# Copying the blocks of u inside DRAM into load order, ahead of the pass that uses them

## The chip, the cores and the metric

The kernel runs on one core of one Trainium2 chip. The metric is the device time of one launch in microseconds (us). The engines are named as in the profile: PE multiplies matrices (PEld is its weight load), DVE and ACT are the vector and scalar engines, POOL works on SBUF and issues the indirect transfers, and SP issues all other DMA transfers. The transfers of SP and of POOL run on the same 16 DMA engines.

## What is computed

One decoder layer on 512 tokens of width 2048, in float32: an input projection, a short convolution and a differential attention side by side, an output projection, and then a product-key expert layer. This last part takes most of the time. Every token chooses 16 of 16,384 experts for each of 8 heads, and every expert is one row of `expert_u` and one row of `expert_v`:

```python
def apply(args):
    xb, ib, gb = args
    u = jnp.take(expert_u, ib, axis=0)
    a = jnp.einsum('thkd,td->thk', u, xb)
    w = (jax.nn.gelu(a.astype(jnp.float32), approximate=False) * gb).astype(xb.dtype)
    vv = jnp.take(expert_v, ib, axis=0)
    return jnp.einsum('thk,thkd->td', w, vv)
```

Both tables are 128 MB (16,384 rows of 8 KB).

## The kernel before

**Stages.** In order of time: the modulation vectors and the q and k columns of the input projection; the v columns (`for g in range(2)`, with `turn`); the convolution columns and the attention heads (`conv`, `head`); the output projection, which also prepares the first 12 blocks of u (`u_ahead`); the projection of the queries onto the key halves (the loop over `w_peer_q`, line 701, below called the key projection), with the top-16 selection on DVE; four blocks of the dense pass between the last selections (`u_block(0)` to `u_block(3)`); the spreading of the gates into `g_dram` (lines 899 to 918, with eight more u blocks); and the dense pass.

**The dense pass.** 352 of the 512 tokens are served densely: all 128 blocks of 128 experts are multiplied with all of these tokens. The other 160 tokens are served by gathers: POOL fetches the chosen rows of `expert_u` and `expert_v` by indirect DMA (line 844, 512 KB each, four buffers `gt`), and DVE multiplies and adds them (lines 853 and 869). Both run beside each other; the gathers are paced by the matmuls.

A block e of the dense pass needs u transposed, so that the width lies on the partitions. `u_load` brings the block to SBUF in 8 transfers of 128 KB each, into a tile `ur` in which partition group s (32 partitions) holds columns s*512 to s*512+511 of the rows, four rows to a partition (line 511):

```python
for b in (0, 2):
    for s in range(4):
        nc.sync.dma_start(t[s * 32:(s + 1) * 32, b:b + 2],
                          expert_u[e * P + b * 32:e * P + b * 32 + 64, s * 512:(s + 1) * 512]
                          .rearrange("(b r) d -> r b d", r=32))
```

DVE then transposes 32x32 squares (line 780, `utf`), ACT and DVE split the result into a high and a low part (lines 88 and 89, `ut`), PE runs 48 matmuls of 352 columns (line 792), and 48 more at line 945, where v (`vr`, one transfer of 512 KB for two blocks and a quarter of the width) is split in the same way (`vs`) and multiplied by the weights `W`. There are two tiles `ur`, so one block is loaded while the one before it is transposed.

The first 12 blocks are different: `u_ahead` transposes them during the output projection and stores them in the DRAM tile `u_dram`, from where one transfer of 1 MB brings each to SBUF (line 773).

**What sets the order.** The framework places the instructions of each engine in an order that it works out itself from the dependencies, with a few orders added by hand. SP issues its transfers strictly in this order: one that has to wait for a buffer holds up all behind it. In addition each transfer from SP takes one of eight completion semaphores in turn and waits, where need be, until the transfer before it on the same semaphore has landed, so at most eight are under way.

**Weights in the earlier stages.** `weights` loads a 512 KB tile `wraw` (four buffers), ACT takes the high part (line 88) and POOL the low part (line 89) into `wsp`, and PE uses it. A free `wraw` buffer thus comes from POOL, and SP waits for it.

Of the kernel before, what the change touches and what calls it, by code (L numbers as in the profile page):

```python
# [78 lines left out]
def hymba_peer(tc, x, c, positions, w_ada, b_ada, norm1_g, w_in, conv_w, q_norm_g, k_norm_g,  # L79
# [18 lines left out]
    with ExitStack() as ctx:  # L98
# [1 line left out]
        y_dram = tc.dram_tile([KC, P, T], F32, name="y_dram")  # L100
        x1_dram = tc.dram_tile([KC, P, T], F32, name="x1_dram")
        g_dram = tc.dram_tile([TD // GB, NK, NK, GB], F32, name="g_dram")
        u_dram = tc.dram_tile([NPRE, P, D], F32, name="u_dram")
        h_dram = tc.dram_tile([TG - P, D], F32, name="h_dram")
        a_dram = tc.dram_tile([P, D], F32, name="a_dram")

# [106 lines left out]
        def ada_later(n):  # L213
            for _ in range(n):
                if later:
                    sec, k0 = later.pop(0)
                    ada(sec, k0, 4)
                    if sec == 4:
                        gain_col(1, 4, k0, 4)


        def weights(w, r0, nk, c0, n, behind=None):
# [164 lines left out]
        for g in range(2):  # L387
            banks = [pm() for _ in range(NT)]
            for kq in range(8):
                qkv_mm(banks, 4 + g, kq * 2, (0, KC - 1))  # L390
            for i in range(NT):
                nc.scalar.activation(vv[:, i, g * 512:(g + 1) * 512], banks[i], AF.Copy)
            turn(2 * g)
            turn(2 * g + 1)
            ada_later(ADA_N.pop(0))
# [51 lines left out]
        def conv(cp):  # L447
            got = []
            for g in (1, 2, 0):
                banks = [pm() for _ in range(2)]  # L450
                for kq in range(4):
                    ws = weights(w_in, kq * 512, 4, g * CONV + cp * 256, 256)
                    for k in range(4):
                        kk = kq * 4 + k
                        for n2 in range(2):
                            for n, (a, b) in enumerate(PASSES):
                                nc.tensor.matmul(banks[n2], ws[:, a, k, n2 * P:(n2 + 1) * P], hT[kk][:, b],  # L457
                                                 start=(kk == 0 and n == 0), stop=(kk == KC - 1 and n == 2))
                for n2 in range(2):
                    if g == 1:  # L460
                        cc = at.tile([P, T], F32, name="cc")
                        nc.scalar.activation(cc, banks[n2], AF.Copy)
                        got.append(cc)
                        continue
                    chn = cp * 2 + n2
                    if g == 2:
                        z = at.tile([P, T + 2], F32, name="cz", bufs=1)
                        nc.vector.memset(z[:, 0:2], 0.0)
                        nc.vector.tensor_tensor(out=z[:, 2:], in0=banks[n2], in1=got[n2], op=OP.mult)
                        y = got[n2]  # L470
                        nc.vector.tensor_scalar(y, z[:, 0:T], ccol[:, 16 + chn:17 + chn], None, op0=OP.mult)
                        for j in (1, 2):
                            wc = ccol[:, 16 + j * 8 + chn:17 + j * 8 + chn]
                            nc.vector.scalar_tensor_tensor(y, z[:, j:T + j], wc, y, op0=OP.mult, op1=OP.add)
                    else:
                        y = got[n2]
                        nc.vector.tensor_tensor(out=y, in0=banks[n2], in1=y, op=OP.mult)
                        nc.sync.dma_start(y_dram[chn], y)
# [210 lines left out]
        for g in range(4):  # L689
            banks = [pm() for _ in range(4)]  # L690
            for kq in range(8):
# [2 lines left out]
                    dense_tokens((g * 8 + kq) * 2 + n, weights.hi)  # L694
                if kq % 2:
                    gathered_tokens((g * 8 + kq) // 2, weights.hi)
                for k in range(2):
                    kk = kq * 2 + k
                    for j in range(4):
                        for n, (a, b) in enumerate(PASSES):  # L700
                            nc.tensor.matmul(banks[j], ws[:, a, k, j * P:(j + 1) * P], h2T[kk][:, b],  # L701
                                             start=(kk == 0 and n == 0), stop=(kk == KC - 1 and n == 2))
# [63 lines left out]
        def u_turn(n):  # L766
# [2 lines left out]
                return  # L769
            if q == 0:  # L770
                UR[0] = up.tile([P, 4, 512], F32, name="ur", bufs=UR_BUFS)
                if e < NPRE:
                    nc.sync.dma_start(UR[0].rearrange("p b d -> p (b d)"), u_dram[e])
                else:
                    u_load(UR[0], e)
            if e < NPRE:
                t = UR[0][:, 2 * q:2 * q + 2].rearrange("p a (c b r) -> p (a c) b r", c=4, b=4)
            else:
# [5 lines left out]
        def u_block(e, behind=None):  # L784
# [15 lines left out]
            if e % 2 == 0:  # L800
# [6 lines left out]
                else:  # L807
                    GE[e // 2] = up.tile([P, 2, TD], F32, name="ge", bufs=GE_BUFS)
            nc.scalar.activation(GE[e // 2][:, e % 2], pa[:, :TD], AF.Gelu)

        held = [scores(qs, i, psV.tile([P, T], F32, name="pv"), gp.tile([P, D // 2], F32, name="gt", bufs=GBUF)[:, 0:T])
                for i in range(NT)]
# [14 lines left out]
            split(W[e // 2], ge)  # L827

        for i in range(NT):
            u_block(i)  # L830
            select(i, 3, held[i])
            finish_select(i)
        tk_ctx.close()
# [63 lines left out]
        with tc.tile_pool(name="gs", bufs=2, side="right") as gs:  # L897
# [3 lines left out]
            for b in range(nb_):  # L901
                gt_ = gs.tile([P, NK, GB], F32, name="gtile")
                for t4 in range(0, GB, 4):
# [12 lines left out]
                        gm = nc.tensor.matmul(pg[:, j], oh[:, 1, j], og[:, j], start=True, stop=True)  # L916
                    nc.scalar.activation(gt_[:, :, t4:t4 + 4], pg.rearrange("p t n -> p n t"), AF.Copy)
                nc.sync.dma_start(g_dram[b], gt_)
                if b >= nb_ - (RUN - NT):
                    u_block(RUN - nb_ + b, behind=gm if b == nb_ - 1 else None)  # L920

# [133 lines left out]
```

## Time and profile before

| | us |
|---|---|
| median of 3 runs (range) | 3523.54 (3519.87 to 3523.54) |
| the profiled execution | 3524.61 |
| span of its instructions | 3522.6 |
| q and k projection, up to | 283 |
| v columns | 283 to 389 |
| convolution and heads | 389 to 772 |
| output projection | 772 to 974 |
| key projection | 974 to 1190 |
| u blocks 0 to 3, last selections | 1190 to 1284 |
| spreading of the gates, u blocks 4 to 11 | 1284 to 1432 |
| dense pass | 1432 to about 3390 |
| end | to 3522 |

How to read it: 2.0 us of the profiled execution lie outside the span. Busy time is time in which an engine executed something; the DMA share is the mean busy share of the 16 DMA engines, and can exceed 1 a little when packets of two queues overlap on an engine. The stage borders come from the first and last matmul of each line.

### The profile page before, as it was taken

What the parts mean: (1) busy time and instruction counts of PE and PEld (TensorE: products, weight loads), DVE (VectorE), ACT (ScalarE), POOL (GpSimd) and SP (SyncE); (2) the same over time, 40 slices, a digit from 0 to 9 for tenths busy, and PEclk for the clock granted to TensorE, in tenths of its full rate; (3) what the DMA queues carried; (4) which work ended last, traced back from release to release, by engine and by line L of the source; (5) the groups of instructions that cost most, each with busy time, mean ns of one, the idle gap of its engine ahead of it and who ended that gap; (6) DMA issues with size and microseconds to landing.
All of it is one profiled execution on the core that took longest, in us unless ns stands there. A gap on an engine that the chain in (4) does not pass through costs nothing.

```text
span 3522.6 us, 49092 instructions
## 1 busy us (share of the span) xinstructions
PE 3223.4 (92%) x18006; PEld 2970.3 (84%) x18006; DVE 2847.1 (81%) x4261; ACT 1220.5 (35%) x1828; POOL 1417.5 (40%) x985
## 2 busy tenths in 40 slices
PE   5888999999998797999999999999999999999985
PEld 4766777677787686899998999889999999999975
DVE  6789766653269999789898888888999898988885
ACT  5232334343264357423232232223233232332221
POOL 2447332254447420134443444333434444444441
PEclk9999999999999899999999999999999999999987
DMA  8864755559722135899999999999999999999984
GB/s 288 286 229 143 254 190 178 183 177 290 252 88 68 61 122 202 264 298 323 305 315 295 310 310 299 300 287 300 306 314 313 298 307 306 326 310 319 299 302 163
DMA packets 425712, 896.34 MB, mean 254 GB/s; under 512 B 40402, under 2 KB 119167, under 8 KB 420735
## 3 DMA queue, kind: packets, MB, share of 16 engines
q1 hardware_dynamic: 333310, 557.62, 52.3%
q0 software_dynamic: 92160, 335.59, 29.3%
q8 instruction: 141, 2.31, 0.3%
q14 instruction: 101, 0.82, 0.1%
HBM read 843.47 MB, written 49.55 MB: 254 GB/s over the span
## 4 chain that ended last, share of the span: by engine, by line
DMA 42%; DVE 28%; PE 15%; issue 9%; POOL 3%; SPq 2%; ACT 1%; DVEq 0%; POOLq 0%; ACTq 0%
DMA ur<-in_expert_u_dram 14%; DMA vr<-in_expert_v_dram 9%; DMA gt<-in_expert_u_dram,idxu 6%; PE pm L457 4%; DMA ada_w<-in_w_ada_dram 4%; DMA gt<-in_expert_v_dram,idxu 4%; DVE gacc L869 3%; DVE utf L780 3%; DVE vs L89 2%; DVE gt L907 2%; DVE gt L853 2%; DVE ut L89 2%; DVE ada_acc L196 2%; PE pm L547 2%; DVE run L196 2%
## 5 line engine op out<-in xcount | busy, mean ns | idle before, releaser
L792 PE MATMUL pa<-hd,ut 128*128 128x352 f32 x6144 | 1077.3, 328 | 63.9 <-DVE ut L89 41.0
L945 PE MATMUL pv<-W,vs 128*128 128x352 f32 x6144 | 1071.4, 328 | 50.6 <-DVE vs L89 27.0
L792 PEld LDWEIGHTS pa<-hd,ut 128*128 128x128 f32 x6144 | 1015.2, 191 | 75.8 <-DVE ut L89 48.4
L945 PEld LDWEIGHTS pv<-W,vs 128*128 128x128 f32 x6144 | 1014.5, 191 | 61.2 <-DVE vs L89 32.7
L89 POOL TENSOR_TENSOR wsp<-wraw,wsp 128x1024 fp32r<-128x1024 f32 x160 | 391.5, 2449 | 562.1 <-ACT wsp L88 530.3
L844 POOL DMA_INDIRECT gt<-in_expert_u_dram,idxu x256 | 343.9, 1344 | 626.4 <-DVE gt L853 309.8
L88 ACT ACTIVATE vs<-vr 128x1024 fp32r<-128x1024 f32 x256 | 271.3, 1060 | 819.2 <-DMA vr<-in_expert_v_dram 365.8
L844 POOL DMA_INDIRECT gt<-in_expert_v_dram,idxu x256 | 340.0, 1328 | 477.9 <-DVE gacc L869 341.5
L853 DVE SCALAR_TENSOR_TENSOR gt<-gt,h2n 128x1024 f32<-128x1024 f32 x320 | 386.2, 1215 | 104.9 <-DMA gt<-in_expert_u_dram,idxu 84.8
L869 DVE SCALAR_TENSOR_TENSOR gacc<-gt,ga_a,gacc 128x1024 f32<-128x1024 f32 x316 | 400.4, 1275 | 73.9 <-DMA gt<-in_expert_v_dram,idxu 48.5
L89 DVE TENSOR_TENSOR vs<-vr,vs 128x1024 fp32r<-128x1024 f32 x256 | 309.8, 1210 | 46.9 <-ACT vs L88 46.7
L88 ACT ACTIVATE ut<-utf 128x1024 fp32r<-128x1024 f32 x232 | 244.0, 1056 | 282.3 <-DVE utf L780 169.6
L780 DVE STREAM_TRANSPOSE utf<-ur 128x1024 f32<-128x1024 f32 x232 | 286.9, 1237 | 18.2 <-DMA ur<-in_expert_u_dram 14.1
L88 ACT ACTIVATE wsp<-wraw 128x1024 fp32r<-128x1024 f32 x160 | 169.1, 1058 | 368.1 <-issue 94.7
L89 DVE TENSOR_TENSOR ut<-utf,ut 128x1024 fp32r<-128x1024 f32 x232 | 281.9, 1215 | 9.6 <-ACT ut L88 9.5
L457 PE MATMUL pm<-big,wsp 128*128 128x512 f32 x1152 | 287.6, 402 | 0.0
L457 PEld LDWEIGHTS pm<-big,wsp 128*128 128x128 f32 x1152 | 215.2, 192 | 42.6 <-issue 0.2
L196 DVE SCALAR_TENSOR_TENSOR ada_acc<-ada_w,scol,ada_acc 128x512 f32<-128x512 f32 x195 | 208.3, 1068 | 28.5 <-DMA ada_w<-in_w_ada_dram 25.1
L245 PE MATMUL pqk<-wsp,big 128*128 128x512 f32 x768 | 193.3, 411 | 21.3 <-DVE qk L291 12.9
L701 PE MATMUL pm<-big,wsp 128*128 128x512 f32 x768 | 188.2, 402 | 16.1 <-POOL wsp L89 14.5
L245 PEld LDWEIGHTS pqk<-wsp,big 128*128 128x128 f32 x768 | 150.6, 199 | 57.6 <-DVE qk L291 15.9
L701 PEld LDWEIGHTS pm<-big,wsp 128*128 128x128 f32 x768 | 146.2, 193 | 48.5 <-POOL wsp L89 17.0
(274 smaller groups left out, 3195.4 us busy)
## 6 DMA issues: line engine op xcount, KB each, us to landing
vr<-in_expert_v_dram SPq DMA_DIRECT2D x256, 512.0 KB, 10.0
ur<-in_expert_u_dram SPq DMA_DIRECT2D x928, 128.0 KB, 9.2
ada_w<-in_w_ada_dram SPq DMA_DIRECT2D x192, 512.0 KB, 4.6
wraw<-in_w_in_dram SPq DMA_DIRECT2D x96, 512.0 KB, 5.0
g_dram<-gtile SPq DMA_DIRECT2D x11, 2048.0 KB, 7.1
g<-g_dram SPq DMA_DIRECT2D x32, 704.0 KB, 13.6
wraw<-in_w_out_dram SPq DMA_DIRECT2D x32, 512.0 KB, 5.1
wraw<-in_w_peer_q_dram SPq DMA_DIRECT2D x32, 512.0 KB, 3.7
```

The source lines that it names most:

```text
L88: hi = nc.scalar.activation(dst[:, 0], src, AF.Copy)
L89: (eng or nc.vector).tensor_tensor(out=dst[:, 1], in0=src, in1=dst[:, 0].bitcast(F32), op=OP.subtract)
L196: nc.vector.scalar_tensor_tensor(new, wt[:, k], s, old, op0=OP.mult, op1=OP.add)
L245: nc.tensor.matmul(banks[i], hT[kk][:, a, i * P:(i + 1) * P], ws[:, b, k], start=(kk == last[0] and n == 0), stop=(kk == last[1] and n == 2))
L457: nc.tensor.matmul(banks[n2], ws[:, a, k, n2 * P:(n2 + 1) * P], hT[kk][:, b], start=(kk == 0 and n == 0), stop=(kk == KC - 1 and n == 2))
L701: nc.tensor.matmul(banks[j], ws[:, a, k, j * P:(j + 1) * P], h2T[kk][:, b], start=(kk == 0 and n == 0), stop=(kk == KC - 1 and n == 2))
L780: nc.vector.transpose(t, UR[0][:, :, q * 256:(q + 1) * 256].rearrange("p b (c r) -> p c b r", r=32))
L792: mm = nc.tensor.matmul(pa[:, :TD], ut[:, a, j], hd[k][:, b], start=(k == 0 and n == 0), stop=(k == KC - 1 and n == 2))
L844: d = nc.gpsimd.indirect_dma_start(out=t, out_offset=None, in_=src, in_offset=bass.IndirectOffsetOnAxis(ap=gidx[g][:, j:j + 1], axis=0), e ...
L853: nc.vector.scalar_tensor_tensor(t, t, 1.0, h2n[:, f * D // 2:(f + 1) * D // 2], op0=OP.mult, op1=OP.mult, accum_out=ga_a[:, f, j:j + 1])
L869: nc.vector.scalar_tensor_tensor(gacc[:, s], t, a, gacc[:, s], op0=OP.mult, op1=OP.add)
L945: mm = nc.tensor.matmul(pv[j // 2][:, j % 2, :TD], vs[:, a, bb, j * P:(j + 1) * P], W[e0 // 2][:, m, bb], start=(b == 0 and n == 0), stop= ...
```

## The change

Every block of u from number 12 on is copied inside DRAM into `u_dram`, in the order in which `ur` holds it, by four transfers of 256 KB (`lay_out`). The dense pass then loads it with one transfer of 1 MB, in which each of the 128 partitions takes one contiguous row of 8 KB. What DVE, ACT and PE do with it afterwards stays as it was.

The 116 copies are spread over the earlier stages: 8 blocks in the v columns, 24 in the convolution stage, 48 in the key projection, 20 in the four u blocks, 16 in the spreading of the gates. Each is placed behind an instruction of that stage by an order that only the scheduler sees; on the chip it waits for nothing but its completion semaphore.

```diff
-        u_dram = tc.dram_tile([NPRE, P, D], F32, name="u_dram")
+        u_dram = tc.dram_tile([NK, P, D], F32, name="u_dram")
...
+        lay = list(range(NPRE, NK))
+
+        def lay_out(n, behind):
+            for _ in range(n):
+                e = lay.pop(0)
+                for s in range(4):
+                    t = nc.sync.dma_start(u_dram[e, s * 32:(s + 1) * 32].rearrange("r (b d) -> r b d", b=4),
+                                          expert_u[e * P:(e + 1) * P, s * 512:(s + 1) * 512]
+                                          .rearrange("(b r) d -> r b d", r=32))
+                    tc.add_manual_dep(t.ins, behind.ins.name, ORDER, reason="weights first")
...
                 qkv_mm(banks, 4 + g, kq * 2, (0, KC - 1))
+                lay_out(kq % 2, weights.hi)
...
                     ws = weights(w_in, kq * 512, 4, g * CONV + cp * 256, 256)
+                    lay_out(kq % 2, weights.hi)
...
                     gathered_tokens((g * 8 + kq) // 2, weights.hi)
+                lay_out(1 + kq % 2, weights.hi)
...
-                if e < NPRE:
-                    nc.sync.dma_start(UR[0].rearrange("p b d -> p (b d)"), u_dram[e])
-                else:
-                    u_load(UR[0], e)
+                nc.sync.dma_start(UR[0].rearrange("p b d -> p (b d)"), u_dram[e])
...
         for i in range(NT):
-            u_block(i)
+            mm = u_block(i)
+            lay_out(5, mm)
...
                 nc.sync.dma_start(g_dram[b], gt_)
+                lay_out(min(2 if b % 2 else 1, len(lay)), gm)
```

What this does to the queue of SP is seen at three places. The first is the key projection, early in its first quarter: `wraw` is a weight tile on its way in, `kr` the keys, `h_dram<-hb` a small store. Before, weight tiles and small transfers follow each other:

```order
L224 DMA wraw_7695<-in_w_peer_q_dram 128x2x512
L606 DMA kr_7258<-in_sub_keys1_dram 128x128
L224 DMA wraw_7726<-in_w_peer_q_dram 128x2x512
L606 DMA kr_7263<-in_sub_keys2_dram 128x128
L224 DMA wraw_7766<-in_w_peer_q_dram 128x2x512
L639 DMA h_dram_64<-hb_7344 32x128
```

Now 8 or 12 copies stand behind every one or two weight tiles (`u_dram<-in_expert_u_dram`, line 228, 256 KB each):

```order
L236 DMA wraw_7835<-in_w_peer_q_dram 128x2x512
L236 DMA wraw_7883<-in_w_peer_q_dram 128x2x512
L620 DMA kr_7386<-in_sub_keys1_dram 128x128
L228 DMA u_dram_63<-in_expert_u_dram 128x1x512 x12
L236 DMA wraw_7918<-in_w_peer_q_dram 128x2x512
L620 DMA kr_7391<-in_sub_keys2_dram 128x128
L236 DMA wraw_7966<-in_w_peer_q_dram 128x2x512
L228 DMA u_dram_63<-in_expert_u_dram 128x1x512 x8
```

The weight tiles and the keys have moved behind copies. The second place is SP at the end of the key projection, where the loads of the first u blocks (`ur<-u_dram`) begin. Before, six of them stood in a row behind the last small store:

```order
L639 DMA h_dram_64<-hb_9065 32x128
L773 DMA ur_9420<-u_dram_63 128x2048
L773 DMA ur_9453<-u_dram_63 128x2048
L773 DMA ur_9588<-u_dram_63 128x2048
L773 DMA ur_9733<-u_dram_63 128x2048
L773 DMA ur_9878<-u_dram_63 128x2048
```

Now 24 copies stand between the last weight tile and the first load, 40 ahead of the fourth load, and 20 ahead of the fifth:

```order
L236 DMA wraw_9364<-in_w_peer_q_dram 128x2x512
L228 DMA u_dram_63<-in_expert_u_dram 128x1x512 x21
L653 DMA h_dram_64<-hb_9294 32x128
L228 DMA u_dram_63<-in_expert_u_dram 128x1x512 x3
L653 DMA h_dram_64<-hb_9377 32x128
L787 DMA ur_9740<-u_dram_63 128x2048
L787 DMA ur_9773<-u_dram_63 128x2048
L787 DMA ur_9928<-u_dram_63 128x2048
L228 DMA u_dram_63<-in_expert_u_dram 128x1x512 x40
L787 DMA ur_10093<-u_dram_63 128x2048
L228 DMA u_dram_63<-in_expert_u_dram 128x1x512 x20
L787 DMA ur_10258<-u_dram_63 128x2048
```

The fourth and fifth loads have moved behind fifteen blocks of copies. The third place is SP in the middle of the dense pass (`vr` is a piece of v, `g4` the gates of four blocks). Before:

```order
L935 DMA vr_17594<-in_expert_v_dram 128x2x512
L511 DMA ur_18155<-in_expert_u_dram 32x2x512 x8
L935 DMA vr_17626<-in_expert_v_dram 128x2x512
L935 DMA vr_17662<-in_expert_v_dram 128x2x512
L935 DMA vr_17694<-in_expert_v_dram 128x2x512
L511 DMA ur_18236<-in_expert_u_dram 32x2x512 x8
```

Now:

```order
L950 DMA vr_17561<-in_expert_v_dram 128x2x512
L787 DMA ur_18036<-u_dram_63 128x2048
L950 DMA vr_17597<-in_expert_v_dram 128x2x512
L950 DMA vr_17629<-in_expert_v_dram 128x2x512
L950 DMA vr_17664<-in_expert_v_dram 128x2x512
L787 DMA ur_18110<-u_dram_63 128x2048
```

Eight rows of 32 partitions each have become one of 128, at about the same places between the pieces of v.

More of the change, by code (lines that the diff above doesn't have):

```diff
@@ L809, in u_block @@
             nc.scalar.activation(GE[e // 2][:, e % 2], pa[:, :TD], AF.Gelu)
+            return mm
         held = [scores(qs, i, psV.tile([P, T], F32, name="pv"), gp.tile([P, D // 2], F32, name="gt", bufs=GBUF)[:, 0:T])
```

## The prediction

> **What bounds the kernel now.** I read the page first: which engine is busy, and what ended last.
>
> ```profile
> PE 3223.4 (92%) x18006; PEld 2970.3 (84%) x18006; DVE 2847.1 (81%) x4261; ACT 1220.5 (35%) x1828; POOL 1417.5 (40%) x985
> DMA 42%; DVE 28%; PE 15%; issue 9%; POOL 3%; SPq 2%; ACT 1%; DVEq 0%; POOLq 0%; ACTq 0%
> ```
>
> PE is busy 92% of the span, yet the chain that ended last runs 42% through transfers. The two agree only if the limits differ by stage, so the second view is the table by stretches, cut at the stage borders (columns: length, busy time and count of PE, PEld, DVE, ACT, POOL, granted clock, DMA share, GB/s).
>
> ```profile
> 283.00:389.00 106.00, 97.63 (x429) 79.68 (x428) 98.58 (x95) 25.06 (x33) 64.56 (x36) 0.95 0.60 192
> 389.00:772.00 383.00, 368.89 (x1700) 278.99 (x1699) 247.87 (x397) 154.11 (x339) 129.59 (x58) 0.98 0.60 192
> 772.00:974.00 202.00, 192.45 (x892) 157.95 (x890) 61.61 (x98) 65.00 (x99) 88.78 (x40) 0.99 0.81 254
> 974.00:1190.00 216.00, 200.78 (x939) 166.13 (x940) 179.77 (x744) 113.02 (x168) 127.91 (x107) 0.96 0.20 64
> 1190.00:1284.00 94.00, 72.66 (x411) 69.99 (x410) 88.76 (x318) 37.20 (x46) 31.07 (x37) 0.89 0.30 111
> 1284.00:1432.00 148.00, 120.95 (x867) 111.15 (x866) 139.74 (x185) 110.67 (x274) 0.00 (x0) 0.98 0.48 179
> 1432.00:1600.00 168.00, 162.77 (x997) 161.61 (x996) 135.21 (x166) 53.53 (x59) 53.86 (x44) 0.99 0.95 300
> 1600.00:3380.00 1780.00, 1707.14 (x10384) 1690.46 (x10383) 1587.62 (x1717) 531.50 (x597) 766.85 (x568) 0.98 1.02 307
> ```
>
> In the dense pass (last two rows) three engines are nearly full at once: PE 96%, DVE 89%, and the DMA share is 1.02. Ahead of it, from 974 to 1432, the DMA engines are mostly idle (0.20, 0.30, 0.48) while PE and DVE work. The change moves DMA work from the last row into these.
>
> The third view groups the dense stretch (1600 to 3380) by line: PE's matmuls, with the idle time ahead of them and what ended it, the reading of `vr` on ACT, and one step of the gathers on POOL and DVE.
>
> ```profile
> L792 PE MATMUL pa<-hd,ut 128*128 128x352 f32 x5242 | 910.2, 326 | 40.5 <-DVE ut L89 20.8 <-ACT ut L88 19.5
> L945 PE MATMUL pv<-W,vs 128*128 128x352 f32 x5142 | 891.1, 326 | 32.4 <-DVE vs L89 18.7 <-ACT vs L88 8.7 <-ACT W L88 3.0
> L869 DVE SCALAR_TENSOR_TENSOR gacc<-gt,ga_a,gacc 128x1024 f32<-128x1024 f32 x284 | 360.0, 1274 | 56.0 <-DMA gt<-in_expert_v_dram,idxu 48.5 <-DMA gt<-in_expert_v_dram,ib 6.7
> L844 POOL DMA_INDIRECT gt<-in_expert_v_dram,idxu x256 | 340.0, 1328 | 477.9 <-DVE gacc L869 341.5 <-DMA gt<-in_expert_v_dram,idxu 40.8 <-issue 35.5
> L88 ACT ACTIVATE vs<-vr 128x1024 fp32r<-128x1024 f32 x214 | 226.8, 1060 | 697.8 <-DMA vr<-in_expert_v_dram 334.7 <-PE pv L945 262.1 <-issue 27.0
> ```
>
> PE waits for splits (`ut`, `vs`), never for a transfer directly. But DVE and ACT, which make the splits in a fixed order, stand still for transfers: DVE for gathered rows, ACT for `vr`. The DMA view of the same stretch gives the landing times (last column, us).
>
> ```profile
> q0 software_dynamic: 81829, 297.95, 52.0%
> q1 hardware_dynamic: 165472, 246.03, 49.9%
> ...
> ur<-in_expert_u_dram SPq DMA_DIRECT2D x856, 128.0 KB, 9.4
> ...
> gt<-in_expert_v_dram,idxu POOLq DMA_INDIRECT x256, 9.4
> gt<-in_expert_u_dram,idxu POOLq DMA_INDIRECT x213, 9.4
> ...
> gt<-in_expert_u_dram,ib POOLq DMA_INDIRECT x64, 9.1
> ...
> gt<-in_expert_v_dram,ib POOLq DMA_INDIRECT x35, 8.2
> ```
>
> The gathers are a ring of four buffers: 568 of them in 1780 us is 3.13 us each, so a buffer comes round every 12.5 us. Its own work is 1.3 (POOL) + 9.4 (landing) + 1.3 (DVE) = 12.0 us. The ring has almost no slack, and three quarters of it is landing time on full DMA engines.
>
> **Part 1: the load of a block gets cheaper.** The price in DMA time has two rows. From 1341 to 1346 us nearly nothing but the old loads (32 partitions each, pieces of 2 KB) was under way:
>
> ```profile
> q1 hardware_dynamic: 746, 1.22, 105.7%
> ```
>
> From 1260 to 1270 us there was just one load from `u_dram` (128 partitions, rows of 8 KB):
>
> ```profile
> q1 hardware_dynamic: 144, 1.05, 28.3%
> ```
>
> Old: 1.057 x 5 us / 1.22 MB x 1.049 MB = 4.5 us of all 16 engines for a block. New: 0.283 x 10 = 2.8 us. That is 1.7 us less. 856/8 = 107 blocks are loaded in the long stretch: 182 us of its 1.02 x 1780 = 1816 us of DMA time, which leaves a share of 0.92, or 0.96 if the stretch shrinks to PE's 1707 us.
>
> What it can bring: PE's idle time, 40.5 + 32.4 = 72.9 us there and 168 - 162.8 = 5.2 us in the stretch ahead, together 78 us. Then PE is the bound, with DVE (1588 of 1707) next. What comes late next is known: at 0.96 transfers still queue, and 31.2 of the 72.9 us ended on ACT, part of which is the fixed order of its work. I take two thirds, **-50 us**; bounds -78 and +10, the latter because the scheduler now orders DVE's splits and gathers a little differently and one such order can be worse.
>
> SP issues one transfer for eight. The row of the old loads in the trace, min/median/max ns of an issue:
>
> ```profile
> L511 SPq DMA_DIRECT2D ur<-in_expert_u_dram x928: 311/419/3407, 1319.3 to 3351.9; - x186
> ```
>
> Eight times 0.42 us becomes one, and with eight semaphores in turn, one block no longer uses up all of them. I put nothing on this beyond the 50 us: the pieces of v behind the loads come earlier, and that is one of the ways in which the 50 us arise.
>
> **Part 2: the copies.** 116 blocks, four transfers each. No transfer in the trace goes from DRAM to DRAM, so the price is bounded from two sides. Loads of 2 KB rows to 128 partitions filled the queue from 45 to 200 us:
>
> ```profile
> q1 hardware_dynamic: 24624, 45.09, 87.4%
> ```
>
> 0.874 x 155 us / 45.09 MB = 3.0 us per MB, 3.15 us for a block. The other side is a store, one `gtile` alone from 1358 to 1372 us:
>
> ```profile
> q1 hardware_dynamic: 144, 2.10, 35.7%
> ```
>
> 0.357 x 14 / 2.10 = 2.4 us per MB, 2.5 us for a block. If an engine reads and writes a copy at the same time, as it must for a load, it costs what the slower side does: 3.15 us. If the two sides share one path, it costs their sum: 5.65 us. I take **3.6 us**, near the load, which has the same 2 KB pieces over all 16 engines, with something for two sides in DRAM.
>
> Now stage by stage, with free DMA time from the table above (length times one minus share):
>
> - v columns: 106 x 0.40 = 42 us free, 8 x 3.6 = 29 needed.
> - convolution: 383 x 0.40 = 153 free, 24 x 3.6 = 86 needed.
> - key projection: 216 x 0.80 = 173 free, 48 x 3.6 = 173 needed.
> - u blocks 0 to 3: 94 x 0.70 = 66 free, 20 x 3.6 = 72 needed.
> - spreading of the gates: 148 x 0.52 = 77 free, 16 x 3.6 = 58 needed.
>
> So the copies fit in three stages, fill the key projection to the brim, and exceed the u blocks by 6 us. Issuing costs nothing visible: 192 copies at 0.42 us are 81 us of SP's 216 in the key projection.
>
> What is queued behind the copies on SP is the next weight tile, for which ACT, POOL and at last PE wait. The cover in the key projection:
>
> ```profile
> PE pm L701 <- POOL wsp L89: 14.5, 5, 4.6
> ```
>
> ```profile
> wraw<-in_w_peer_q_dram SPq DMA_DIRECT2D x25, 512.0 KB, 3.8
> ```
>
> PE waits 14.5 us in all for a split weight, so POOL is only just ahead. PE uses a tile in 216/32 = 6.75 us, and four buffers give some 20 us of warning; a tile behind eight copies lands after 8 x 0.9 + 3.8 = 11 us. That hides as long as the engines keep up on average, and at 3.6 us they have no reserve, because SP also stands still for a free buffer while copies behind it could run. I put 10 us on this and 5 us on the same effect in the earlier stages, whose buffers have more cover. Sum of part 2: 0 + 6 + 10 + 5 = **+21 us**. Bounds: at 3.15 us some 8 us; at 5.65 us (271 - 173) + (113 - 66) + (90 - 77) + (45 - 42) + 15 = 176 us.
>
> A load from `u_dram` needs its copy landed. Block 12 is needed after about 1310 us and copied before 389; the last 16 blocks are copied until 1432 and needed after 3100. No wait there.
>
> **Sum.** 3524.6 (span 3522.6 and 2.0 around it) - 50 + 21 = 3495.6 us for the profiled execution; the median of the runs lies 1.1 us under that execution, so 3495 us.
>
> **Rivals.**
>
> *A. The copies cost nearer to read plus write, and the key projection becomes bound by DMA (slower).* The place is the key projection and the u blocks behind it. From 4.0 us a block this eats the whole gain: 68 x 4.0 - 239 + 15 = 48 us. At 4.8 us, the middle of what lies above: 57 + 30 + 15 = 102 us, so 3495 + (102 - 21) = 3576 us. For it: no row shows that one engine can read and write DRAM at once. Against it: a load also passes an engine in and out, and reaches 3.0 us per MB. Chance 0.32.
>
> The Trainium skill has a price for this, in "DMA: Bandwidth & Descriptors", section "Latency and other measured facts": copies between DRAM tensors in tiles of 16 KB rows reached 207 to 214 GB/s per direction. Worked out from it, an estimate: 4.9 us for a block, 110 us for the stages and about 3583 us in all; the page does not say whether the tiles went through SBUF, and no trace here shows such a copy.
>
> *B. The dense pass does not shorten.* If gathers land no earlier, their ring still needs 12.0 of 12.5 us, DVE stands as before, and the pass gains perhaps 15 us: 3524.6 - 1.1 - 15 + 21 = 3530 us. For it: a gather is 512 KB in pieces on the same engines, whatever SP sends. Against it: 9.4 us on engines that are full must be mostly queue, and the old loads land in 9.4 us there for a quarter of the bytes. Chance 0.08.
>
> *C. Everything fits.* PE becomes the bound and the copies cost 3.15 us: -78 + 8, 3454 us. Chance 0.08.
>
> **How the numbers follow.** The forecast case (a copy under 4.0 us, a gain of 30 to 70 us, 3463 to 3518 us) has 0.52. With C that makes 0.60 for faster. About 0.2%, 7 us, is what a measurement of this kernel can tell from no change; within it lie 0.06 of B and 0.01 of A. Slower: 0.31 of A and 0.02 of B. The range reaches down to 3450, just under C, and up to 3590, where a copy costs 5.1 us; I leave out 0.13 above and 0.03 below.
>
> **What would show it.** Right: the DMA share of the dense pass at 0.92 to 0.97, gathers landing in 8.5 us or less, PE's idle time there under 35 us, the key projection at most 15 us longer. The direct test is the DMA time of the copies in the convolution stage: 3.6 us a block or not. Wrong: a DMA share of 1 from 974 to 1432 us with PE waiting for `wsp` and `ut` (A), or gathers still landing in 9.4 us (B).

## The result, and the profile after

The changed kernel takes 3419.2 us (median of four runs, 3404.9 to 3427.2) against 3521.7 us (3518.5 to 3523.5) of the kernel before, run beside it: a ratio of 0.9708, interval 0.9684 to 0.9732. The forecast was 3495 us in a range from 3450 to 3590. The sign was right, the gain is more than three times the forecast one (102 us instead of 29), and the time lies below the range.

The profiled execution took 3427.2 us. From the page of the changed kernel, PE's line and the chain that ended last:

```profile
PE 3189.8 (93%) x18006; PEld 2950.5 (86%) x18006; DVE 2840.9 (83%) x4261; ACT 1219.8 (36%) x1826; POOL 1419.2 (41%) x985
PE 39%; DVE 15%; DMA 11%; issue 6%; POOL 2%; ACT 0%; SPq 0%; DVEq 0%; ACTq 0%; POOLq 0%
```

Transfers were 42% of the chain and are 11% now; PE was 15% and is 39%. PE does the same 18006 matmuls, but its busy time has shrunk too, by 34 us. That second fact matters below.

The table by stretches of the changed kernel, cut at its own stage borders (length, busy time and count of PE, PEld, DVE, ACT, POOL, granted clock, DMA share, GB/s):

```profile
283.00:393.00 110.00, 98.64 (x429) 80.25 (x430) 95.34 (x96) 27.05 (x36) 66.99 (x39) 0.94 0.70 233
393.00:766.00 373.00, 365.37 (x1701) 277.26 (x1700) 253.14 (x405) 155.05 (x340) 135.96 (x59) 0.99 0.83 272
...
965.00:1186.00 221.00, 203.25 (x941) 167.63 (x942) 182.29 (x748) 114.17 (x170) 125.91 (x107) 0.95 0.89 279
1186.00:1280.00 94.00, 51.26 (x268) 47.61 (x267) 91.48 (x319) 31.06 (x47) 28.90 (x37) 0.75 0.81 263
1280.00:1428.00 148.00, 136.46 (x1013) 131.68 (x1012) 139.32 (x179) 113.29 (x270) 0.00 (x0) 1.00 0.93 337
...
1600.00:3290.00 1690.00, 1669.77 (x10296) 1662.15 (x10296) 1574.90 (x1706) 527.48 (x591) 775.69 (x570) 1.00 0.91 322
```

The DMA work has moved as the diff says: the share in the key projection (third row shown) went from 0.20 to 0.89, in the u blocks from 0.30 to 0.81, in the spreading of the gates from 0.48 to 0.93, and fell from 1.02 to 0.91 in the dense pass. The stages that took it on are as long as before (in brackets), within 5 us, or shorter: 110 (106), 373 (383), 221 (216), 94 (94), 148 (148).

Where the time went is read from the matmuls of the dense pass: L792 and L945 of the kernel before, L804 and L960 of the changed one, are its u half and its v half. The rows give the shortest, median and longest time of an instruction in ns, then the first and the last start in us. Before:

```profile
L792 PE MATMUL pa<-hd,ut x6144: 317/323/662, 1194.3 to 3389.2; 128*128 128x352 f32 x199
L945 PE MATMUL pv<-W,vs x6144: 317/323/662, 1446.5 to 3510.2; 128*128 128x352 f32 x199
```

After:

```profile
L804 PE MATMUL pa<-hd,ut x6144: 317/323/662, 1190.1 to 3301.8; 128*128 128x352 f32 x199
L960 PE MATMUL pv<-W,vs x6144: 317/323/663, 1442.1 to 3412.2; 128*128 128x352 f32 x199
```

The first v matmul starts 4.4 us earlier, although 464 copies were put ahead of it. From there to the end of the span it took 3522.6 - 1446.5 = 2076.1 us and takes 3424.9 - 1442.1 = 1982.8 us: 93.3 us less. The whole gain of 97.7 us of span is these two. Up to the last u matmul it is 3389.2 - 1446.5 = 1942.7 us before and 3301.8 - 1442.1 = 1859.7 after, 83.0 us less. The remaining 10.3 us lie behind that matmul, where 28 steps of `gacc` were still to be done and now 23 are: the gathers were further on by then.

The dense stretch (1600 to 3290) of the changed kernel by line, with busy time, mean ns, idle time ahead and what ended it:

```profile
L804 PE MATMUL pa<-hd,ut 128*128 128x352 f32 x5179 | 894.5, 325 | 13.1 <-DVE ut L89 12.0 <-ACT ut L88 1.1
L960 PE MATMUL pv<-W,vs 128*128 128x352 f32 x5117 | 874.1, 323 | 7.1 <-ACT W L88 5.0 <-DVE vs L89 1.3 <-ACT vs L88 0.5
L883 DVE SCALAR_TENSOR_TENSOR gacc<-gt,ga_a,gacc 128x1024 f32<-128x1024 f32 x288 | 362.5, 1276 | 27.4 <-DMA gt<-in_expert_v_dram,idxu 18.8 <-DMA gt<-in_expert_v_dram,ib 8.3
L88 ACT ACTIVATE vs<-vr 128x1024 fp32r<-128x1024 f32 x213 | 225.8, 1060 | 579.7 <-PE pv L960 527.1 <-issue 38.1 <-DMA vr<-in_expert_v_dram 6.6
```

And its transfers there:

```profile
q0 software_dynamic: 81803, 297.88, 49.3%
q1 hardware_dynamic: 112004, 244.44, 40.9%
...
vr<-in_expert_v_dram SPq DMA_DIRECT2D x213, 512.0 KB, 7.0
ur<-u_dram SPq DMA_DIRECT2D x106, 1024.0 KB, 7.7
...
gt<-in_expert_v_dram,idxu POOLq DMA_INDIRECT x256, 6.8
gt<-in_expert_u_dram,idxu POOLq DMA_INDIRECT x210, 7.0
```

ACT waited 334.7 us for `vr` and waits 6.6; it is PE now that ACT waits for. DVE waited 56.0 us for gathered rows at `gacc` and waits 27.4. PE's idle time fell from 72.9 to 20.2 us. A gather lands in 6.9 us instead of 9.4, so the ring of four needs 1.3 + 6.9 + 1.3 = 9.5 us of the 4 x 1690 / 570 = 11.9 us in which a buffer comes round.

### The profile page after: what moved, and what is told of

It is laid out like the page before. It is cut to its first block, busy times and chain, and to the rows that moved or that the text cites. A ratio compares the mean times of both kernels' runs of the same rounds, so it can differ in the third digit from the quotient of the medians.

```text
span 3424.9 us, 48472 instructions
## 1 busy us (share of the span) xinstructions
PE 3189.8 (93%) x18006; PEld 2950.5 (86%) x18006; DVE 2840.9 (83%) x4261; ACT 1219.8 (36%) x1826; POOL 1419.2 (41%) x985
## 3 DMA queue, kind: packets, MB, share of 16 engines
q0 software_dynamic: 92160, 335.59, 27.4%
## 4 chain that ended last, share of the span: by engine, by line
PE 39%; DVE 15%; DMA 11%; issue 6%; POOL 2%; ACT 0%; SPq 0%; DVEq 0%; ACTq 0%; POOLq 0%
PE pa L804 18%; PE pv L960 18%; DMA gt<-in_expert_u_dram,idxu 5%; DVE gt L867 2%; DMA gt<-in_expert_v_dram,ib 2%; PE pv L930 2%; DMA u_dram<-in_expert_u_dram 2%; DVE vs L89 1%; DVE utf L792 1%; DVE ut L89 1%; DVE gt L921 1%; DVE gacc L883 1%; POOL gt L858 1%; DVE tkj L691 1%; PE pm L561 1%
## 5 line engine op out<-in xcount | busy, mean ns | idle before, releaser
L804 PE MATMUL pa<-hd,ut 128*128 128x352 f32 x6144 | 1078.3, 327 | 41.9 <-DVE ut L89 32.3
L960 PE MATMUL pv<-W,vs 128*128 128x352 f32 x6144 | 1058.2, 325 | 20.6 <-ACT W L88 10.1
L804 PEld LDWEIGHTS pa<-hd,ut 128*128 128x128 f32 x6144 | 1010.2, 190 | 48.1 <-DVE ut L89 36.6
L960 PEld LDWEIGHTS pv<-W,vs 128*128 128x128 f32 x6144 | 1004.0, 189 | 26.9 <-ACT W L88 11.9
L792 DVE STREAM_TRANSPOSE utf<-ur 128x1024 f32<-128x1024 f32 x232 | 287.2, 1240 | 0.1
L196 DVE SCALAR_TENSOR_TENSOR ada_acc<-ada_w,scol,ada_acc 128x512 f32<-128x512 f32 x195 | 201.1, 1031 | 42.5 <-DMA ada_w<-in_w_ada_dram 38.8
```

What stands on the lines that cost most here:

```text
L196: nc.vector.scalar_tensor_tensor(new, wt[:, k], s, old, op0=OP.mult, op1=OP.add)
L792: nc.vector.transpose(t, UR[0][:, :, q * 256:(q + 1) * 256].rearrange("p b (c r) -> p c b r", r=32))
L804: mm = nc.tensor.matmul(pa[:, :TD], ut[:, a, j], hd[k][:, b], start=(k == 0 and n == 0), stop=(k == KC - 1 and n == 2))
L960: mm = nc.tensor.matmul(pv[j // 2][:, j % 2, :TD], vs[:, a, bb, j * P:(j + 1) * P], W[e0 // 2][:, m, bb], start=(b == 0 and n == 0), stop= ...
```

## The experiments

All ratios are against runs of the kernel before made beside them. The first four kernels share one set of these (median 3526.8 us), the next four another (3529.4), the last two a third (3522.9). The last columns are of the stretch from 1700 to 3250 us of each profile: matmuls done there, DMA share, and landing time of the gathers by `idxu` from v (empty where the trace gives none, or where the dense pass is shifted too far to compare).

| kernel | us | ratio (interval) | matmuls | DMA | gather |
|---|---|---|---|---|---|
| before | 3521.7 | 1 | 9069 | 1.03 | 9.4 |
| the change | 3419.2 | 0.9708 (0.9684 to 0.9732) | 9497 | 0.91 | 6.8 |
| copies_only | 3513.7 | 0.9955 (0.9929 to 0.9982) | 8954 | 1.03 | 9.3 |
| loads_only | 3416.1 | 0.9699 (0.9660 to 0.9738) | 9589 | 0.92 | 7.0 |
| four_narrow_direct | 3576.2 | 1.0144 (1.0085 to 1.0203) | 8771 | 1.02 | 10.1 |
| eight_wide | 3393.9 | 0.9647 (0.9606 to 0.9688) | 9630 | 0.94 | 6.9 |
| change_again | 3413.9 | 0.9675 (0.9637 to 0.9713) | 9537 | 0.91 | 7.0 |
| eight_wide_again | 3392.8 | 0.9603 (0.9566 to 0.9640) | 9620 | 0.94 | 6.9 |
| four_wide | 3400.9 | 0.9638 (0.9595 to 0.9681) | 9576 | 0.93 | 7.0 |
| four_narrow_copy | 3602.2 | 1.0223 (1.0172 to 1.0274) | 8700 | 0.99 | 9.6 |
| sixteen_narrow_direct | 3564.2 | 1.0098 (1.0066 to 1.0130) | 8785 | 0.98 | |
| key_copies_doubled | 3614.3 | 1.0236 (1.0182 to 1.0290) | | | |

**The copies alone.** The change's copies are made, but the dense pass loads from the original table, as before:

```diff
-                nc.sync.dma_start(UR[0].rearrange("p b d -> p (b d)"), u_dram[e])
+                if e < NPRE:
+                    nc.sync.dma_start(UR[0].rearrange("p b d -> p (b d)"), u_dram[e])
+                else:
+                    u_load(UR[0], e)
```

> All 116 copies as in the change, but the dense pass loads its blocks from expert_u by eight transfers each, as before the change. The prediction's price of the copies was +21 us. The trace after the change speaks for less: its key projection is 4.5 us longer and its dense pass begins 4 us earlier than before. Expected 3515 to 3530 us if the copies are hidden, 3540 or more if they cost what was predicted and the change only won it back elsewhere. Both theories below expect the dense pass as long as before, about 1943 us from its first matmul on v to its last on u.

It takes 3513.7 us, 13 us less than the kernel before, with a ratio of 0.9955 whose interval ends at 0.9982. So 116 blocks of copies cost nothing that shows. The little that it gains lies ahead of the dense pass, which begins at 1435.8 us, 10.7 us earlier than before; the convolution alone is 9 us shorter between its first and its last matmul. Why is not shown. Where the dense pass ends is no fixed border: it lasts 1971 us up to the last u matmul here, 28 us more than before, but 24 us less follow behind it. The sum of both is the quantity to compare: 2081 us here, 2076 before.

**The new load alone.** The copies are left out, and every block of the dense pass is loaded from one of the twelve that `u_dram` holds anyway:

```diff
-            for _ in range(n):
+            for _ in range(0):
...
-                nc.sync.dma_start(UR[0].rearrange("p b d -> p (b d)"), u_dram[e])
+                nc.sync.dma_start(UR[0].rearrange("p b d -> p (b d)"), u_dram[e % NPRE])
```

> No copies; each block from 12 on is loaded by one transfer of 1 MB from one of the twelve blocks in u_dram, so the numbers of the dense pass are those of other experts. This is the gain of the new load alone. Expected the dense pass at 1860 us as after the change and 3415 to 3430 us in all. If part of the gain came from the copies (from another order of the earlier stages), it ends above 3435 us.

It takes 3416.1 us, as long as the change. The load makes the whole gain. The scheduler has put 323 of DVE's 2027 instructions of the dense pass at other places than in the change, so the gain doesn't hang on one order either.

**What about the load: its DMA time (theory D), or the number of transfers and semaphores (theory S)?** The new load differs in several things at once: one transfer for eight, 128 partitions for 32, another source. Two kernels change one of them each. The first keeps 32 partitions and the original table, with four transfers of 256 KB for eight of 128 KB:

```diff
-                    u_load(UR[0], e)
+                    for s in range(4):
+                        nc.sync.dma_start(UR[0][s * 32:(s + 1) * 32],
+                                          expert_u[e * P:(e + 1) * P, s * 512:(s + 1) * 512]
+                                          .rearrange("(b r) d -> r b d", r=32))
```

> The kernel before, without copies, with each block of the dense pass loaded straight from expert_u by four transfers of 256 KB to 32 partitions each in place of eight of 128 KB; pieces of 2 KB as before. Theory D (DMA time): a transfer to 32 partitions occupies the engines longer for a byte (4.5 against 2.8 us a block), and this is what the change removed. It expects the DMA share still at 1.0, gathers landing in 9 us, and 3505 to 3525 us. Theory S (semaphores): eight transfers a block take all eight completion semaphores in turn and so hold up the pieces of v behind them on SP. It expects half of the gain or more here, 3440 to 3475 us.

The second keeps the change's source and its 128 partitions, and issues eight transfers again, of 1 KB to each partition:

```diff
-                nc.sync.dma_start(UR[0].rearrange("p b d -> p (b d)"), u_dram[e])
...
+                    for h in range(8):
+                        nc.sync.dma_start(UR[0].rearrange("p b d -> p (b d)")[:, h * 256:(h + 1) * 256],
+                                          u_dram[e, :, h * 256:(h + 1) * 256])
```

> The change with each block loaded from u_dram by eight transfers to all 128 partitions, 1 KB each, in place of one. Theory D expects nearly the whole gain to stay, since all partitions are written at once: 3415 to 3445 us, DMA share under 0.95. Theory S expects it lost, since a block takes all eight semaphores again: 3500 to 3525 us, pieces of v landing late and ACT waiting some 300 us for them.

Half as many narrow transfers made it slower, 3576.2 us; eight wide ones made it faster than the change, 3393.9 us. S is refuted twice. D has the sign, but neither number was in its range. SP's waits for transfers to land, on which S rests, don't follow the times either: in the stretch from 1700 to 3250 us they were 609 us before; they are 100 in four_narrow_direct and 30 in four_narrow_copy further down, both slower, 161 in eight_wide_again, the fastest, and none in the change. Of four_narrow_direct, the landing times between 1700 and 3250 us, which were 10.5 for `vr`, 9.6 for `ur` and 9.4 for `gt` before:

```profile
vr<-in_expert_v_dram SPq DMA_DIRECT2D x182, 512.0 KB, 12.4
ur<-in_expert_u_dram SPq DMA_DIRECT2D x364, 256.0 KB, 11.8
...
gt<-in_expert_v_dram,idxu POOLq DMA_INDIRECT x256, 10.1
```

Beside the larger narrow transfers `vr` and the gathers from v land later; the gathers from u do not (9.4 us in both), and `ur` itself is twice as large as before.

**Partitions, or the source?** It was still possible that the old loads are dear because they read scattered pieces of 2 KB (theory R). The deciding pair loads from the copied blocks, in four transfers of 256 KB in both kernels. One sends each to 32 partitions:

```diff
+                    for s in range(4):
+                        nc.sync.dma_start(UR[0][s * 32:(s + 1) * 32].rearrange("p b d -> p (b d)"),
+                                          u_dram[e, s * 32:(s + 1) * 32])
```

> The change with each block loaded from u_dram by four transfers to 32 partitions each, rows of 8 KB. The pieces are as large and as contiguous as in the change; only the partitions that one transfer reaches are fewer. Theory D expects most of the gain lost: DMA share 1.0 in the dense pass, gathers landing in 9 to 10 us, 3500 us or more. If the 2 KB pieces scattered over expert_u were what cost the time before (theory R, reading), the gain stays: 3410 to 3440 us.

The other sends each to all 128:

```diff
+                    for s in range(4):
+                        nc.sync.dma_start(UR[0][:, s], u_dram[e, :, s * 512:(s + 1) * 512])
```

> The change with each block loaded from u_dram by four transfers to 128 partitions, 2 KB each. Theory D (DMA time) expects the gain kept, 3390 to 3430 us. Theory P expects it between the change and eight_wide, nearer to eight_wide. If instead the other order of DVE's work is what makes eight_wide faster, there is no reason for an order among the three.

The narrow one takes 3602.2 us, the wide one 3400.9 us. The source, the bytes and the count are the same, and so is the order of the instructions: of some 2027 on DVE in the dense pass one stands elsewhere, on PE, ACT and SP none. The pieces differ, 8 KB in the narrow one and 2 KB in the wide one, but 8 KB pieces to 128 partitions are the change itself, 3413.9 us. So some 200 us hang on how many partitions one transfer reaches. R is refuted: the narrow one reads whole rows of 8 KB, the most orderly source of all, and is the slower. The chain to PE shows in the same pair: from 1700 to 3250 us DVE waits 216 us for gathers in the narrow one and 31 in the wide one, and PE is idle for 102 us and for 5. In the stretch from 1700 to 3250 us, the queue of loads and two landing times of four_narrow_copy:

```profile
q1 hardware_dynamic: 99129, 207.88, 50.0%
...
vr<-in_expert_v_dram SPq DMA_DIRECT2D x180, 512.0 KB, 9.4
...
gt<-in_expert_v_dram,idxu POOLq DMA_INDIRECT x256, 9.6
```

The same of four_wide:

```profile
q1 hardware_dynamic: 147435, 228.98, 43.8%
...
vr<-in_expert_v_dram SPq DMA_DIRECT2D x202, 512.0 KB, 7.2
...
gt<-in_expert_v_dram,idxu POOLq DMA_INDIRECT x256, 7.0
```

The wide one moves more bytes in less engine time: 0.438 x 1550 / 228.98 = 2.97 us per MB, 3.1 us for a block. If the other loads of the narrow kernel cost that as well, its 364 x 0.262 = 95.4 MB of `ur` took 0.500 x 1550 - 112.5 x 2.97 = 441 us, 4.6 us per MB and 4.8 us for a block. But the others cost more there, too. The trace has every packet with its size, and nearly all packets of 8 KB are `ur` in this kernel: they took 4.2 us of all engines per MB, 4.4 us for a block, and the packets of 2 KB took 3.2 us per MB. In the change the packets of 8 KB took 2.6 us per MB, 2.7 us for a block. The Trainium skill says in "SBUF — State Buffer", section "Door 1: The DMA port swizzle (why `[64,N]` ≈ `[32,N]`)", that the rate depends on how many of 16 ports the partitions reach, and that 32 partitions reach eight, with an asymptote of 218 GB/s: an estimate from it is 4.8 us for a block, and these runs come near it with 4.4. What the rows add to it is that the others pay as well: gathers that have nothing to do with these loads land in 9.6 instead of 7.0 us.

**Sixteen narrow transfers.** If a run of narrow transfers to one group of partitions clogs the rest, smaller ones that go round the four groups in turn should help:

```diff
-                    u_load(UR[0], e)
+                    for b in range(4):
+                        for s in range(4):
+                            r0 = e * P + b * 32
+                            nc.sync.dma_start(UR[0][s * 32:(s + 1) * 32, b],
+                                              expert_u[r0:r0 + 32, s * 512:(s + 1) * 512])
```

> The kernel before, without copies, with each block loaded straight from expert_u by sixteen transfers of 64 KB to 32 partitions each, the four partition groups in turn after every transfer. Four transfers of 256 KB were slower than eight of 128 KB. If that is because a long run of pieces for one group of 32 partitions keeps all engines on the same partitions, shorter runs mix the groups better and this one is faster than before: 3440 to 3500 us. Theory S (semaphores) expects it slower than before, since a block takes all eight semaphores twice: 3530 us or more. If only the bytes to 32 partitions count, it equals before within 15 us.

It takes 3564.2 us, ratio 1.0098: slower, where mixing had promised 3440 to 3500 us. Yet the engine time did fall. The queue of loads in the same stretch, with four, eight (the kernel before) and sixteen narrow transfers for a block:

```profile
q1 hardware_dynamic: 135281, 210.03, 52.0%
q1 hardware_dynamic: 144802, 216.67, 50.5%
q1 hardware_dynamic: 152014, 210.36, 46.5%
```

That is 3.84, 3.61 and 3.43 us of all engines per MB, so smaller narrow transfers were cheaper to move in these kernels. What makes this kernel slow is another thing, and SP's waits point to it (us in total, times, longest). Before:

```profile
SPq L511 <- DMA vr<-in_expert_v_dram: 290.0, 98, 5.4
SPq L511 <- DVE utf L780: 209.3, 73, 8.2
```

With sixteen transfers:

```profile
SPq L778 <- DMA vr<-in_expert_v_dram: 260.4, 118, 4.8
SPq L778 <- DMA ur<-in_expert_u_dram: 184.2, 345, 2.8
SPq L778 <- DVE utf L784: 63.3, 22, 7.5
```

SP waits for transfers to land about as long as before (574 us in all, 609 before). But it hardly waits for a free buffer any more, 106 us against 508: it has twice as many loads of u to issue, is seldom ahead, and the blocks come late. DVE's reordering of a block, which waited 11.9 us in all before:

```profile
L784 DVE STREAM_TRANSPOSE utf<-ur 128x1024 f32<-128x1024 f32 x183 | 226.7, 1239 | 134.6 <-DMA ur<-in_expert_u_dram 100.8 <-DMA vr<-in_expert_v_dram 24.9 <-DMA h2n<-h_dram 5.4
```

So the number of transfers can matter after all, as S expected here (3530 us or more), but at sixteen for a block. Four narrow ones cost more engine time than eight; whether that alone makes them slower stays open, since the order of the instructions differs between these kernels as well (397 of DVE's 2025).

**Eight wide transfers against one.** The surprise of the first set was tried again beside the change itself.

> The change itself, for comparison on the same chip with the three that follow: one load of 1 MB to 128 partitions in rows of 8 KB. Expected 0.965 to 0.975 of the kernel before, PE idle some 20 us in the dense stretch.

> Eight loads of 128 partitions by 1 KB a block once more, beside the change on one chip. If small pieces let the gathers' packets through sooner (theory P, packets), it is again 15 to 30 us under the change. If the first difference came from the chips (the intervals nearly touch), it is within 8 us of it.

Its median is 21.1 us under the change, and no run of one reaches the other's (3386.8 to 3395.7 against 3409.4 to 3422.4). Eight transfers of 128 KB are better than one of 1 MB here. DVE's waits for gathers from u in the change (change_again):

```profile
L867 DVE SCALAR_TENSOR_TENSOR gt<-gt,h2n 128x1024 f32<-128x1024 f32 x239 | 286.3, 1214 | 33.4 <-DMA gt<-in_expert_u_dram,idxu 25.3 <-DMA gt<-in_expert_u_dram,ib 7.9
```

With eight transfers (eight_wide_again):

```profile
L872 DVE SCALAR_TENSOR_TENSOR gt<-gt,h2n 128x1024 f32<-128x1024 f32 x241 | 289.3, 1215 | 10.8 <-DMA gt<-in_expert_u_dram,idxu 7.7 <-DMA gt<-in_expert_u_dram,ib 2.5
```

The theory was that short transfers let gathers pass between them. DVE does wait less, and the order one, four, eight is that of the medians. With four, DVE's order is the change's but for 3 instructions, and its waits for gathers, those at `gacc` counted in, fell from 57.4 to 30.8 us; that speaks for the theory. But the median landing of a gather is the same (7.0 and 6.9 us), the interval of four overlaps both, and in the kernel with eight 302 of DVE's 2027 instructions stand elsewhere. That eight beat one is shown; why is not.

**The copies past the capacity.** Rival A said that the key projection stretches once its copies need more than the free DMA time. Each copy there is made twice, the second into a DRAM tile that nobody reads:

```diff
+                    if twice:
+                        t = nc.sync.dma_start(u_two[e, s * 32:(s + 1) * 32].rearrange("r (b d) -> r b d", b=4),
...
-                lay_out(1 + kq % 2, weights.hi)
+                lay_out(1 + kq % 2, weights.hi, twice=True)
```

> The change with every copy of the key projection made twice (the second to a tile that nothing reads), 96 blocks of copies there in place of 48. In the trace after the change a copied block takes about 3.4 us of the DMA engines there. If that price holds, the stage needs 96 x 3.4 + 45 = 371 us of its 221 and gets about 150 us longer, with PE waiting for split weights: 3560 to 3590 us. If the copies run beside the rest more cheaply than their busy time says, it gets under 100 us longer.

3614.3 us. The key projection lasts 411 us, 193 more than in the change, and the dense pass behind it is as long as in the change (1854 us, against 1860 and 1854 in its two profiles). The queue from 965 to 1360 us:

```profile
q1 hardware_dynamic: 58484, 105.82, 91.4%
```

0.914 x 395 = 361 us, less 44 for 28 weight tiles, over 348 copies (87 blocks): 3.6 us for a block. What PE waits for, from 965 to 1390 us:

```profile
ACT wsp L88 <- DMA wraw<-in_w_peer_q_dram: 233.5, 7, 44.3
...
PE pm L722 <- ACT wsp L88: 166.0, 6, 31.4
```

A weight tile waits up to 44 us behind copies, and PE with it. That is rival A's mechanism, with twice the copies. It came out 24 to 54 us dearer than the 3560 to 3590 us expected: 48 blocks more at 3.6 us are 173 us of all engines, and at a share of 0.914 these take 189 us, near the 193 measured.

## Why the prediction was right and wrong

**The mechanism was right.** Narrow loads overfill the DMA engines in the dense pass, the gathers land late, their ring runs dry, DVE and ACT stand, PE waits. Of the signs named ahead, gathers landing in 8.5 us or less (6.9), PE idle under 35 us (20.2) and a key projection at most 15 us longer (4.5 by its first and last matmul) came true; the DMA share of 0.92 to 0.97 came out at 0.91. The prices of a block held, too: 4.4 us to 32 partitions and 2.7 to 128 by the packets, where the prediction had 4.5 and 2.8. Rival B is out. The direction was thus right for the reason that was given; the size was not, in two terms that missed the same way.

**The first failed step: "I take two thirds, -50 us; bounds -78 and +10".** It was 83 us up to the last u matmul and 93 us with the end. The bound itself was wrong, because it took PE's idle time as all there is to gain and its busy time as fixed. Compare the same 1650 us in both kernels. Before:

```profile
1600.00:3250.00 1650.00, 1584.23 (x9640) 1569.10 (x9639) 1473.41 (x1601) 493.93 (x554) 711.06 (x527) 0.98 1.03 307
```

After:

```profile
1600.00:3250.00 1650.00, 1629.77 (x10047) 1622.15 (x10047) 1536.29 (x1671) 514.67 (x577) 756.63 (x557) 1.00 0.91 323
```

One matmul took 1650 / 9640 = 171.2 ns and takes 164.2. Of these 6.9 ns, idle time makes 6.8 - 2.0 = 4.8; the other 2.1 are busy time, 164.3 ns for a matmul before and 162.2 after, at a granted clock of 0.98 and 1.00. At this rate 1942.7 us become 1942.7 x 9640 / 10047 = 1864 us, 79 of the 83 us: about 55 from idle time and 24 from faster matmuls. Where the second part comes from is seen at one stall of the kernel before, in which PE stands still for 6.9 us until ACT has split a piece of `vr` that landed late. The 16 us with the stall, the 16 us behind it, and three parts of the first:

```profile
1902.00:1918.00 16.00, 9.11 (x40) 8.82 (x39) 11.21 (x16) 2.82 (x4) 4.19 (x4) 0.68 1.01 273
1918.00:1934.00 16.00, 16.00 (x101) 16.00 (x100) 14.02 (x20) 5.28 (x6) 5.78 (x6) 1.00 1.04 300
...
1906.00:1910.00 4.00, 0.00 (x0) 0.00 (x0) 2.36 (x3) 0.00 (x0) 0.93 (x1) 0.68 1.08 271
1910.00:1914.00 4.00, 2.52 (x9) 2.52 (x10) 2.54 (x4) 1.76 (x3) 0.00 (x0) 0.50 1.04 252
1914.00:1918.00 4.00, 4.00 (x16) 4.00 (x16) 4.00 (x6) 1.06 (x1) 1.27 (x2) 0.54 0.91 218
```

40 matmuls stand against 101: 61 / 101 x 16 = 9.7 us are lost for 6.9 us of idle time, since the granted clock falls to 0.50 in the stall and stays there for some us while PE is busy again. The Trainium skill has this rule in "TensorE: Matmul & The Clock Gate", section "What's actually happening": an idle window of about 3.4 us halves the clock, a busy one restores it. The rows agree, with 0.50 behind an idle time of 6.9 us. A ceiling from idle time alone is therefore too low when stalls are of this length. The two thirds themselves were near: PE's idle time fell by some 70%, worth 55 us where 50 stood. What the term left out is the 24 us of busy time. In eight_wide_again the idle time is nearly gone:

```profile
1700.00:3250.00 1550.00, 1548.79 (x9620) 1548.16 (x9620) 1470.71 (x1575) 490.21 (x551) 715.14 (x531) 1.00 0.94 329
```

That is 161.1 ns for a matmul, the pace at which PE is the bound.

**The second failed step: "Sum of part 2: 0 + 6 + 10 + 5 = +21 us".** The price under it was near. In the convolution the queue of loads stood, before (389 to 772), at

```profile
q1 hardware_dynamic: 49605, 73.37, 59.7%
```

and after (393 to 766), with 24 blocks of copies, at

```profile
q1 hardware_dynamic: 64973, 101.18, 82.5%
```

0.825 x 373 - 0.597 x 383 = 79 us more for 27.8 MB more. 25.2 MB of it are the copies; the other 2.6, at 3.0 us per MB, took 8 us: 71 / 24 = 3.0 us a block. In the key projection (965 to 1186):

```profile
q1 hardware_dynamic: 34141, 61.50, 89.0%
```

197 us, less 41 for 26 weight tiles and 6 for two loads from `u_dram`, over 176 copies (44 blocks): 3.4 us. So a copy costs what a load costs while the engines have room, and 3.4 to 3.6 us where they don't; 3.6 was assumed. Rival A's point of 4.0 us was not reached in any run as engine time; but with copies in excess the engines were 91% busy, and at that share 3.6 us of them fill 3.9 us of a stage. The estimate of 4.9 us worked out from the Trainium skill's page "DMA: Bandwidth & Descriptors", section "Latency and other measured facts", is too high for these copies: 1.049 MB in 3.9 us are some 270 GB/s written and as much read.

What was mis-sized are the waits. The 10 us for weight tiles behind copies: PE waits for `wsp` in the key projection were 14.5 us and are

```profile
PE pm L716 <- POOL wsp L89: 15.4, 5, 5.6
```

though a tile now lands in 6.9 us instead of 3.8. The cover of four buffers held; the stage is 4.5 us longer. The 6 us of the u blocks: they were late, as forecast, but PE did their matmuls in the next stage, which had room: 411 matmuls in the u blocks became 268, and 867 in the spreading became 1013. DVE, busy 91.5 of 94 us, sets that stage's length. The 5 us of the earlier stages did not show either. The convolution is even 10 us shorter, and that goes with the copies: from its first to its last matmul it takes 370 to 375 us in the eight kernels that have them and 379 to 383 in the four others. Whether the copies or the order of instructions that came with them do it, no run shows. The starts of the dense pass lie at 1444.1 to 1452.8 us in the four profiles without the copies (before, loads_only, four_narrow_direct, sixteen_narrow_direct) and at 1435.8 to 1447.9 in the seven with the change's own copies, so nothing of +21 is left.

**A part not foreseen** is the 10 us at the end, put at nothing in the sum.

Put together for the profiled execution: the dense pass -83 instead of -50, the stages ahead -4 instead of +21, the end -10 instead of 0. That makes -98, by rounded figures, instead of -29. Rival C, in which everything fits, was the nearest in kind and had 0.08; its 3454 us still had the too narrow ceiling in it. The range ended at 3450 for the same reason.

## What to carry to other kernels

In this kernel a transfer that reached few partitions took the engines' time from all others; a block was best loaded across all 128, even at the price of a second copy in DRAM, since stages with idle DMA engines could pay for it. When a wait on the critical path is to be priced, count the matmuls done per us with and without stalls, not PE's idle time: the stall of 6.9 us above cost 9.7, its own length and the slow clock behind it. And before a wait is charged to a stage, ask which engine sets the stage's length and whether the next stage has room for the work that comes late.

## What the runs showed of the hardware

Copies from DRAM to DRAM in pieces of 2 KB cost little more engine time than loads: 3.0 to 3.6 us per block of 1.049 MB, read and write together, by the sums above. Loads of the same blocks cost 2.7 to 3.1 us to 128 partitions and 4.4 us to 32, and the narrow ones raise the landing of gathers beside them from 7.0 to 9.6 us. Eight transfers of 128 KB to 128 partitions beat one of 1 MB by 21 us in a pass of some 1850 us, although they used more engine time (a DMA share of 0.94 against 0.91). Where copies were in excess, their queue held the engines 91% of the time, not 100%.
